# A hybrid decoder trunk: the weights' rings in a pool of their own, between the constants and the slots

## The chip, the core and the metric

The kernel runs on one core of a Trainium2 chip. The metric is the device time of one execution in microseconds (us), the median of several runs. All arithmetic is in float32 or in float32r, a form of float32 with fewer bits that most of its matmuls use.

## What is computed

Two layers over 512 tokens of width 1024. Each layer normalises x, projects it (indexer, attention, gated linear attention and pooling share one projection), mixes three branches, projects back, and runs a gated feed-forward block with a causal convolution of width 3. Cut to what matters here:

```python
def hybrid_layer(x, ...):
    h = rms_norm(x, norm1_g)
    proj = h @ w_in
    ...
    o_a = dsa_attention(qa, ka, va, qi, ki, wi)      # top 128 keys of an indexer, then softmax
    o_b = gla_chunked(qb, kb, vb, log_a)             # gated linear attention, norm, swish gate
    o_c = multiscale_pool(uc, w_pool, pool_scale)
    x = x + jnp.concatenate([o_a, o_b, o_c], axis=-1) @ w_out
    x = x + conv_glu_ffn(rms_norm(x, norm2_g), w_up, conv_w, conv_b, w_down)
    return x

def conv_glu_ffn(x, w_up, conv_w, conv_b, w_down):   # D_FF = 2816
    h = x @ w_up
    a, b = h[..., :D_FF], h[..., D_FF:]
    ...                                              # conv = causal convolution of a
    return (jax.nn.silu(conv) * b) @ w_down
```

By far the largest part of the arithmetic is the products with the weight matrices `w_in`, `w_out`, `w_up` and `w_down`, in two layers.

## The kernel before

Activations lie transposed: 128 partitions by 512 columns, one column per token, a tile (a "slot") for each 128 of the 1024 features. A product of full float32 precision is made of three float32r matmuls: weight and activation are each split into a high part and a remainder, and `mm3` issues high x high, high x remainder and remainder x high into the same PSUM bank. In the names of the profile the weights' parts are `hi` and `lo`; the activations' parts are `xh` and `xl`, or `h` and `l`. A row that says `mm<-xh,hi` is such a matmul. PSUM tiles `mm` take these products (four banks), tiles `aux` all smaller ones.

`Kern.weights` brings one weight block in: a DMA from the SP queue into `raw` (up to 1024 columns of 4 bytes in each partition), an ACT copy that rounds it to `hi`, and a DVE subtraction that makes `lo`. The three kinds of tile are rings: 3 buffers of `raw`, 5 of `hi`, 5 of `lo` (`NRAW`, `NW`). A block of 1024 columns is eight slices of 128 columns, so that a slice, 512 bytes in each partition, is what TensorE loads as its stationary operand:

```python
out.append((hi[:, kk, :].bitcast(F32R), lo[:, kk, :].bitcast(F32R)))
```

`Kern.chunk` then makes 128 output features of all 512 tokens: eight times `mm3`, with a weight slice stationary and a slot of 512 columns moving. `w_down` does the same inside `layer` and `finish`. In `Kern.tokens` (the value projection `w_v` and the 340 columns of `w_tok`) the roles are exchanged: a slice of the activations is stationary, and the weights move.

Only the first products of the first layer, `w_qi` and `w_gqk`, take their weights from another place: `run` loads them into ordinary slots, named `first` (raw), `fh` and `fl` (the parts), half as wide as the rings' tiles. Those slots have the same size as the slots of the activations.

The order of the work on each engine is made ahead by a planner in the kernel (`Plan.schedule`), from a cost for each operation, and written out. It knows tiles by name and by the number of buffers of their kind. It does not know addresses.

Where a tile lies in SBUF follows from the pools. A pool places its kinds of tile one after another, in the order of their first use, and the pools follow each other: `cst` (constants), then `sl` (everything else). The first constants start 128 bytes past a multiple of 512, and the pool's odd sizes end at 34,304 = 67 x 512. In `sl` come 50 slots of 2048 bytes, some small tiles, the four `tb` temporaries, two tiles `small` of 1344 bytes, and then the three rings, then the `ta` temporaries and the remaining small tiles. In bytes of a partition:

| tiles | start | past a multiple of 512 |
|---|---|---|
| slots (activations, `first`, `fh`, `fl`) | 34,304 | 0 |
| `raw` ring, 3 x 4096 | 152,960 | 384 |
| `hi` ring, 5 x 4096 | 165,248 | 384 |
| `lo` ring, 5 x 4096 | 185,728 | 384 |
| `ta` temporaries, 4 x 2048 | 206,208 | 384 |

So each weight slice of 512 bytes begins 384 bytes past a multiple of 512, and each slot at a multiple of 512.

Of the kernel before, what the change touches and what calls it, by code (L numbers as in the profile page):

```python
# [11 lines left out]
F32 = mybir.dt.float32  # L12
# [6 lines left out]
P = 128  # L19
# [75 lines left out]
NSLOT, NRAW, NW, NMM = 50, 3, 5, 4  # L95
# [21 lines left out]
class Op:  # L117
    __slots__ = ("eng", "cost", "calls", "preds", "succs", "tiles", "func", "tags", "port", "shapes")

    def __init__(self, eng):  # L120
        self.eng, self.cost, self.calls = eng, 0.0, []
        self.preds, self.succs, self.tiles, self.func, self.tags = {}, {}, set(), None, set()
        self.port, self.shapes = False, []
# [370 lines left out]
class Kern:  # L494
    def __init__(self, ctx, tc, a):
        self.tc, self.nc, self.a = tc, tc.nc, a
        e = ctx.enter_context
        self.pl = Plan(tc.nc)
        self.cst = e(tc.tile_pool(name="cst", bufs=1))
        self.sl = e(tc.tile_pool(name="sl", bufs=1))  # L500
        self.dr = e(tc.tile_pool(name="dr", bufs=1, space=bass.MemoryType.DRAM))
        self.ps = e(tc.tile_pool(name="ps", bufs=1, space=bass.MemoryType.PSUM))
        self.n = 0
# [29 lines left out]
    def weights(self, src, k, n, whole=False):  # L533
        nc = self.pl
        out = []
        step = k if whole else min((k + 1) // 2, 1104 // n)
        for k0 in range(0, k, step):
            kn = min(step, k - k0)
            raw = self.pl.tile(self.sl, NRAW, (P, kn * n), F32, "raw", self.nm("raw"))
            nc.sync.dma_start(out=raw, in_=src[:, k0 * n:(k0 + kn) * n])  # L540
            nc.in_turn("raw")
            hi = self.pl.tile(self.sl, NW, (P, kn, n), F32, "hi", self.nm("hi"))
            lo = self.pl.tile(self.sl, NW, (P, kn, n), F32, "lo", self.nm("lo"))
            hf = hi.rearrange("p k n -> p (k n)")
            lf = lo.rearrange("p k n -> p (k n)")
            nc.scalar.activation(out=hf.bitcast(F32R), in_=raw, func=AF.Copy)
            nc.in_turn("hi")
            nc.vector.tensor_tensor(out=lf.bitcast(F32R), in0=raw, in1=hf, op=OP.subtract)
            nc.in_turn("lo")
            for kk in range(kn):  # L550
                out.append((hi[:, kk, :].bitcast(F32R), lo[:, kk, :].bitcast(F32R)))
        return out
# [871 lines left out]
```

## Time and profile before

| | |
|---|---|
| median of 3 runs | 1260.47 us (1258.75 to 1262.89) |
| the profiled execution | 1258.48 us |
| its span, first to last instruction | 1256.7 us |
| mean granted TensorE clock | 0.997 of full |
| busy: TensorE matmul / VectorE / ScalarE / GpSimd | 99% / 55% / 40% / 26% |
| mean busy share of the DMA engines, hardware queue | 33.1% |

The span is the profiled execution without what lies before its first and after its last instruction, 1.8 us. A matmul's busy time in the profile overlaps that of the next one, and its end is modelled. What a stream of matmuls costs is therefore read from the distance between the starts of neighbours, called the pitch here, and not from the duration of one. All operations are recorded through one helper, so each has line 488, and rows are told apart by their tiles.

Roughly, the span goes: 0 to 31 us loading and the first products; 31 to 220 us attention, gated linear attention and pooling of layer 0, between them its projections; 220 to 640 us output projection and feed-forward block of layer 0; 640 to 840 us and 840 to 1220 us the same of layer 1; 1220 us to the end the last two feature blocks, the final norm and the output.

### The profile page before, as it was taken

How to read it: one execution, taken by the hardware profiler on the slowest of the kernel's cores; microseconds unless marked ns; L12 is line 12 of the kernel's file. 1: busy time of each engine (PE TensorE's matmuls, PEld its weight loads, DVE VectorE, ACT ScalarE, POOL GpSimd, SP SyncE). 2: the span in 40 equal slices, each digit the busy share in tenths (PEclk: the TensorE clock that was granted, in tenths of full speed). 3: DMA queues.
4: the chain of work that ended last, by engine and by line, in shares of the span. 5: the costliest groups of instructions: out<-in, count | busy, mean ns of one | idle time of the engine just before them, and what ended most of it. 6: DMA issues, size and time to landing. Idle time of an engine off the chain costs nothing.

```text
span 1256.7 us, 16776 instructions
## 1 busy us (share of the span) xinstructions
PE 1241.9 (99%) x6254; PEld 1004.3 (80%) x6254; DVE 695.5 (55%) x1256; ACT 508.6 (40%) x824; POOL 331.7 (26%) x281
## 2 busy tenths in 40 slices
PE   8999999999999999999999999999999999999997
PEld 7886678888888888888888777888888888888887
DVE  6569996355554245444357999644554524444333
ACT  6462278443332133333336324863433312333321
POOL 1363251222221022222108422512222200222211
PEclk9999999999999999999999999999999999999998
DMA  7322365122323323224343135432223223222322
GB/s 258 115 78 93 97 166 167 51 85 70 115 63 93 129 84 101 92 69 133 122 156 98 51 124 141 123 118 68 69 99 107 87 92 118 86 90 82 88 75 68
DMA packets 50561, 129.38 MB, mean 103 GB/s; under 512 B 7456, under 2 KB 10800, under 8 KB 50480
## 3 DMA queue, kind: packets, MB, share of 16 engines
q1 hardware_dynamic: 50368, 128.04, 33.1%
q8 instruction: 49, 0.80, 0.3%
q14 instruction: 32, 0.26, 0.1%
q0 software_dynamic: 112, 0.28, 0.1%
HBM read 109.22 MB, written 4.26 MB: 90 GB/s over the span
## 4 chain that ended last, share of the span: by engine, by line
PE 91%; DVE 5%; DMA 2%; issue 1%; ACT 1%; SPq 0%; POOL 0%; DVEq 0%
PE mm L488 81%; PE aux L488 10%; DVE score L488 1%; DVE lo L488 1%; DVE m L488 1%; DVE pl L488 1%; DMA raw<-in_w_tok 1%; DVE qt L488 1%; DMA x<-in_x 1%; SPq L488 0%; DMA raw<-in_w_rb 0%; DVE att L488 0%; DVE out L488 0%; ACT relu L488 0%; DVE u L488 0%
## 5 line engine op out<-in xcount | busy, mean ns | idle before, releaser
L488 PE MATMUL mm<-xh,hi 128*128 128x512 f32 x960 | 385.5, 402 | 0.3 <-DVE q L488 0.3
L488 PE MATMUL mm<-xh,lo 128*128 128x512 f32 x960 | 378.9, 395 | 0.0
L488 PE MATMUL mm<-xl,hi 128*128 128x512 f32 x960 | 378.6, 394 | 0.0
L488 DVE TENSOR_TENSOR lo<-raw,hi 128x1024 fp32r<-128x1024 f32 (+3 forms) x210 | 251.4, 1204 | 197.0 <-ACT hi L488 189.0
L488 ACT ACTIVATE hi<-raw 128x1024 fp32r<-128x1024 f32 (+3 forms) x210 | 203.2, 974 | 384.6 <-PE mm L488 333.4
L488 PEld LDWEIGHTS mm<-xh,hi 128*128 128x128 f32 x960 | 180.8, 188 | 47.6 <-issue 7.5
L488 PEld LDWEIGHTS mm<-xh,lo 128*128 128x128 f32 x960 | 180.7, 188 | 42.5
L488 PEld LDWEIGHTS mm<-xl,hi 128*128 128x128 f32 x960 | 180.9, 188 | 39.4 <-issue 0.2
L488 PE MATMUL mm<-h,hi 128*128 128x512 f32 (+2 forms) x492 | 187.8, 382 | 0.0
L488 PE MATMUL mm<-h,lo 128*128 128x512 f32 (+2 forms) x492 | 186.4, 379 | 0.0
L488 PE MATMUL mm<-l,hi 128*128 128x512 f32 (+2 forms) x492 | 186.3, 379 | 0.0
L488 POOL TENSOR_TENSOR cv<-cv,rstd 128x512 f32<-128x512 f32 x44 | 58.4, 1328 | 309.8 <-ACT cv L488 289.7
L488 POOL TENSOR_TENSOR l<-cv,h 128x512 fp32r<-128x512 f32 x44 | 70.4, 1600 | 157.0 <-ACT h L488 157.0
L488 PEld LDWEIGHTS mm<-h,lo 128*128 128x128 f32 x492 | 92.8, 189 | 18.8
L488 PEld LDWEIGHTS mm<-h,hi 128*128 128x128 f32 x492 | 92.8, 189 | 18.3 <-issue 0.3
L488 PEld LDWEIGHTS mm<-l,hi 128*128 128x128 f32 x492 | 92.9, 189 | 18.0
L488 DVE TENSOR_TENSOR x<-x,mm 128x512 f32<-128x512 f32 (+2 forms) x52 | 33.5, 646 | 103.0 <-PE mm L488 100.0
L488 DVE SCALAR_TENSOR_TENSOR cv<-a,vec,cv 128x511 f32<-128x511 f32 (+1 forms) x88 | 70.4, 806 | 33.5 <-ACT cv L488 32.2
L488 ACT ACTIVATE cv<-a,vec 128x512 f32<-128x512 f32 x44 | 35.6, 813 | 127.7 <-DVE a L488 127.7
L488 DVE TENSOR_TENSOR a<-mm,rstd 128x512 f32<-128x512 f32 x44 | 30.2, 691 | 96.6 <-PE mm L488 96.6
L488 POOL TENSOR_TENSOR sq<-sq,sq 128x512 f32<-128x512 f32 x23 | 34.6, 1506 | 151.2 <-ACT sq L488 151.1
L488 DVE TENSOR_TENSOR cv<-cv,mm 128x512 f32<-128x512 f32 x44 | 30.1, 685 | 41.1 <-PE mm L488 38.6
(199 smaller groups left out, 1393.5 us busy)
## 6 DMA issues: line engine op xcount, KB each, us to landing
raw<-in_w_up SPq DMA_DIRECT2D x88, 512.0 KB, 3.8
raw<-in_w_down SPq DMA_DIRECT2D x32, 384.0 KB, 3.1
raw<-in_w_down SPq DMA_DIRECT2D x32, 320.0 KB, 2.9
raw<-in_w_qk SPq DMA_DIRECT2D x16, 512.0 KB, 3.8
raw<-in_w_out SPq DMA_DIRECT2D x16, 512.0 KB, 4.0
x<-in_x SPq DMA_DIRECT2D x16, 256.0 KB, 6.0
raw<-in_w_v SPq DMA_DIRECT2D x8, 512.0 KB, 4.4
raw<-in_w_rb SPq DMA_DIRECT2D x4, 512.0 KB, 4.8
```

The lines of the kernel that those rows point to most:

```text
L488: self.issued(i, fn(*args, **kw))
```

## The change

The three rings are taken from a pool of their own, `wt`, which is opened between the constants' pool and the slots' pool. Nothing else is changed.

```diff
         self.cst = e(tc.tile_pool(name="cst", bufs=1))
+        self.wt = e(tc.tile_pool(name="wt", bufs=1))
         self.sl = e(tc.tile_pool(name="sl", bufs=1))
...
-            raw = self.pl.tile(self.sl, NRAW, (P, kn * n), F32, "raw", self.nm("raw"))
+            raw = self.pl.tile(self.wt, NRAW, (P, kn * n), F32, "raw", self.nm("raw"))
             nc.sync.dma_start(out=raw, in_=src[:, k0 * n:(k0 + kn) * n])
             nc.in_turn("raw")
-            hi = self.pl.tile(self.sl, NW, (P, kn, n), F32, "hi", self.nm("hi"))
-            lo = self.pl.tile(self.sl, NW, (P, kn, n), F32, "lo", self.nm("lo"))
+            hi = self.pl.tile(self.wt, NW, (P, kn, n), F32, "hi", self.nm("hi"))
+            lo = self.pl.tile(self.wt, NW, (P, kn, n), F32, "lo", self.nm("lo"))
```

The planner's input is the same, so the instructions of every engine stand in the same order as before, with the same waits. Only addresses change:

| tiles | start before | start after | past a multiple of 512, before and after |
|---|---|---|---|
| `raw` ring | 152,960 | 34,304 | 384, 0 |
| `hi` ring | 165,248 | 46,592 | 384, 0 |
| `lo` ring | 185,728 | 67,072 | 384, 0 |
| slots | 34,304 | 87,552 | 0, 0 |
| `tb` temporaries | 141,824 | 195,072 | 0, 0 |
| `ta` temporaries and the small tiles behind them | 206,208 | 206,208 | 384, 384 |

The rings take 53,248 bytes, which is 104 x 512 (and 26 x 2048), so what moves up behind them keeps its place within 512 bytes. The constants stay where they are. The `ta` temporaries stay 384 bytes past a multiple of 512. The slices of `w_tok` are 1360 bytes wide, so that of the three slices in a buffer only the first begins at a multiple of 512 after the change. The slices of all other weights do, whether they are 128, 256 or 512 columns wide.

## Rows read from the trace of the kernel before

**Rows 1.** The page's first part: busy time of each engine.

```profile
PE 1241.9 (99%) x6254; PEld 1004.3 (80%) x6254; DVE 695.5 (55%) x1256; ACT 508.6 (40%) x824; POOL 331.7 (26%) x281
```

**Rows 2.** The page's chain that ended last: shares by engine, then by line.

```profile
PE 91%; DVE 5%; DMA 2%; issue 1%; ACT 1%; SPq 0%; POOL 0%; DVEq 0%
PE mm L488 81%; PE aux L488 10%; DVE score L488 1%; DVE lo L488 1%; DVE m L488 1%; DVE pl L488 1%; DMA raw<-in_w_tok 1%; DVE qt L488 1%; DMA x<-in_x 1%; SPq L488 0%; DMA raw<-in_w_rb 0%; DVE att L488 0%; DVE out L488 0%; ACT relu L488 0%; DVE u L488 0%
```

**Rows 3.** The same chain in order of time: start us, us, what.

```profile
191.76 0.70 PE mm L488 x3
192.57 0.70 PE mm L488 x3
193.73 0.70 PE mm L488 x3
194.43 1.57 PE aux L488 x14
196.00 0.70 PE mm L488 x3
...
272.08 367.18 PE mm L488 x1590
```

**Rows 4.** Windows, mm tiles alone: stretch, length, busy (count touching it) by engine, clock, DMA.

```profile
13.00:21.60 8.60, 8.60 (x40) 7.12 (x39) 0.00 (x0) 0.00 (x0) 1.00 0.98 337
225.00:268.00 43.00, 43.00 (x186) 34.67 (x184) 5.48 (x8) 0.00 (x0) 1.00 0.19 62
273.00:633.00 360.00, 360.00 (x1551) 291.91 (x1550) 40.50 (x59) 0.00 (x0) 1.00 0.31 99
841.00:880.00 39.00, 39.00 (x169) 31.38 (x168) 5.38 (x8) 0.00 (x0) 1.00 0.26 81
884.00:1220.00 336.00, 335.42 (x1444) 271.98 (x1445) 37.75 (x55) 0.00 (x0) 1.00 0.29 91
31.00:220.00 189.00, 132.58 (x549) 96.80 (x549) 11.80 (x20) 4.59 (x8) 1.00 0.41 119
640.00:840.00 200.00, 142.20 (x579) 103.04 (x580) 11.67 (x20) 4.45 (x8) 1.00 0.38 110
```

**Rows 5.** Timeline of PE: start us, us, matmul; rows 1 to 3, 8, 9 and 43.

```profile
402.04 0.40 PE L488 MATMUL mm<-h,lo 128*128 128x512 f32 x1
402.28 0.40 PE L488 MATMUL mm<-h,hi 128*128 128x512 f32 x1
402.52 0.39 PE L488 MATMUL mm<-l,hi 128*128 128x512 f32 x1
...
403.67 0.40 PE L488 MATMUL mm<-h,hi 128*128 128x512 f32 x1
403.91 0.40 PE L488 MATMUL mm<-l,hi 128*128 128x512 f32 x1
...
411.80 0.40 PE L488 MATMUL mm<-h,lo 128*128 128x512 f32 x1
```

**Rows 6.** Timeline of PE, 849 to 854 us: the first and last of 18 rows.

```profile
849.75 0.40 PE L488 MATMUL mm<-xh,lo 128*128 128x512 f32 x1
...
853.72 0.39 PE L488 MATMUL mm<-l,hi 128*128 128x512 f32 x1
```

**Rows 7.** Timeline of PE, 13.3 to 21.5 us: the first and last of 37 rows.

```profile
13.30 0.39 PE L488 MATMUL mm<-xh,fl 128*128 128x512 f32 x1
...
21.46 0.39 PE L488 MATMUL mm<-xh,fl 128*128 128x512 f32 x1
```

**Rows 8.** Timeline of PE after a pause: four of 14 rows (the 1st, 2nd, 11th, 14th).

```profile
24.32 0.49 PE L488 MATMUL mm<-xh,fh 128*128 128x512 f32 x1
24.64 0.40 PE L488 MATMUL mm<-xl,fh 128*128 128x512 f32 x1
...
26.73 0.39 PE L488 MATMUL mm<-xl,fh 128*128 128x512 f32 x1
...
27.41 0.39 PE L488 MATMUL mm<-xl,fh 128*128 128x512 f32 x1
```

**Rows 9.** Groups by form on PE and ACT: xcount | busy us, mean ns | idle before.

```profile
L488 PE MATMUL mm<-xh,hi 128*128 128x512 f32 x960 | 385.5, 402 | 0.3 <-DVE q L488 0.3
L488 PE MATMUL mm<-h,hi 128*128 128x512 f32 x426 | 169.5, 398 | 0.0
L488 PE MATMUL mm<-hi,xh 128*128 128x512 f32 x64 | 26.0, 406 | 0.0
L488 ACT ACTIVATE hi<-raw 128x1024 fp32r<-128x1024 f32 x140 | 147.7, 1059 | 218.0 <-PE mm L488 185.1 <-issue 22.1 <-DMA raw<-in_w_rb 5.5
L488 ACT ACTIVATE hi<-raw 128x640 fp32r<-128x640 f32 x32 | 23.5, 735 | 90.3 <-PE mm L488 73.3 <-issue 16.9
```

**Rows 10.** Tile fh, the ACT copies: xcount: minimum/median/maximum ns.

```profile
L488 ACT ACTIVATE fh<-first x8: 615/617/632, 5.5 to 20.0; 128x512 fp32r<-128x512 f32 x8
```

**Rows 11.** Page, DVE's subtractions (all forms) and the commonest weight DMA.

```profile
L488 DVE TENSOR_TENSOR lo<-raw,hi 128x1024 fp32r<-128x1024 f32 (+3 forms) x210 | 251.4, 1204 | 197.0 <-ACT hi L488 189.0
raw<-in_w_up SPq DMA_DIRECT2D x88, 512.0 KB, 3.8
```

## The prediction

> **What bounds the kernel now.** First the busy times [rows 1]: TensorE is busy for 99% of the span, VectorE for 55%, ScalarE for 40%. A busy TensorE may still be waiting inside its pipeline, so the next view is the chain that ended last [rows 2]. It lies on TensorE for 91%, and 81% of it are the matmuls into the `mm` tiles, the products with the weights. In order of time [rows 3] one piece of that chain is 367.18 us long, 1590 matmuls with nothing between them. There the kernel takes as long as TensorE needs from one matmul to the next, and no other engine has a say. In the attention stretches the same rows show pieces of three matmuls, broken by small products.
>
> So the number to read is the pitch, start to start. The reader is to see three pitches for the same matmul, 128x512 in float32r:
>
> - In the feed-forward block [rows 5], 43 starts in a row span 402.04 to 411.80 us: 9.76 us by 42 is **232.4 ns**. The pitch is not even: 402.04 to 402.28 is 240, most others are 230, and 403.67 to 403.91 is 240 again. It returns every seventh matmul, while high and low parts change every third. Over the four long unbroken stretches [rows 4] it is the same: a count there holds about two matmuls that began before the stretch, so 360.00 us by 1549 is 232.4 and 43.00 by 185 is 232.4.
> - At 850 us [rows 6] the output projection of layer 1 runs at 3.97 us by 17, or 233.5 ns.
> - At the start, where the weights lie in ordinary slots as `fh` and `fl` [rows 7], 37 starts span 13.30 to 21.46 us: 8.16 us by 36 is **226.7 ns**, and that stretch is even.
>
> The rows rule out what would first come to mind. The granted clock is 1.00 in all of these stretches [rows 4], the 2.4 GHz level, so it is not the clock. In 13 to 21.6 us the DMA engines are 98% busy, in the others 19 to 32% [rows 4], so the faster stretch is the one with more traffic. What differs is the place: in the start stretch stationary and moving operand both begin at multiples of 512 bytes, and in the others the weights begin 384 bytes past one. A stream also has a warm-up [rows 8]: after a pause, nine pitches from 24.64 to 26.73 us average 232.2 ns, and then three to 27.41 us average 227. With both operands on the boundary a stream settles after some ten matmuls. With the weights off it, 1549 in a row do not settle.
>
> **The change part by part.** It removes, adds and reorders nothing on any engine or queue, SP's and GpSimd's included. It moves the rings from 384 past a multiple of 512 to 0, and the slots stay at 0. Four things touch the rings.
>
> *Matmuls in the long streams.* The weights' slices then lie as those of the start stretch do. I take its pitch. The four long stretches [rows 4] are 43 + 360 + 39 + 336 = 778 us at 232.4 ns (the third a little more). At 226.7 they would take 778 x 226.7 / 232.4 = 758.9, so 19.1 us less. All of it lies on the path, since the chain is TensorE there [rows 3]. The cover must hold: everything that feeds TensorE must come 2.5% sooner. VectorE has 45% of the span free and ScalarE 60% [rows 1], and a weight DMA lands in 3.8 us [rows 11], where the 48 matmuls of a block of `w_up` (two DMAs) take 48 x 226.7 ns = 10.9 us. Nothing is late next.
>
> The trace has no stream from the rings at a multiple of 512, so I bound this term. The least is 0 (the start stretch is faster for a reason that doesn't move with the rings), and the most is what all 128x512 matmuls of this kind could give. There are (960 + 426 + 64) x 3 = 4350 of them [rows 9], where each group stands for three; by 5.7 ns that is 24.8 us for this term and the next together. I take 19.1, the value of the stretch with the same layout.
>
> *Matmuls in the attention stretches.* There 132.58 + 142.20 = 274.8 us are `mm` work [rows 4]. At most 2.5% of it, 6.8 us, can go; at least 0. The streams there are short [rows 3], and a stream of fewer than ten is as slow with aligned operands [rows 8]. I take a quarter, 1.7 us.
>
> *ScalarE's and VectorE's work on the rings.* An ACT copy into `hi` takes 1059 ns for 1024 columns and 735 for 640 [rows 9], which by the slope of 0.84 ns a column is 627 for 512. The same copy between slots takes 617 [rows 10]. If those 10 ns go, 210 copies give 2 us of ScalarE, which is idle 60% of the time and hidden by TensorE. VectorE's 251.4 us of subtractions [rows 11] could move by as small a share either way, under the same cover. Zero for both. Without that cover, in the attention stretches, they'd be worth at most 2 us each.
>
> *DMAs into `raw`.* 3.8 us for 512 KB [rows 11]. DMA is 2% of the chain [rows 2], all at the start, so even 4% more or less of a transfer is below 1 us. Zero.
>
> Sum: 19.1 + 1.7 = 20.8 us. The profiled execution took 1258.48 us, so 1237.7. The median of the runs stands 2.0 us above that execution, so I forecast **1239.7 us**, 1.6% faster.
>
> **A rule that speaks against it.** The rows say that the pitch of one and the same instruction is 226.7 or 232.4 ns at one clock, and that the place of its operands is what I find different [rows 5, 7]. The Trainium skill, page "SBUF — State Buffer", section "Who interferes with whom", gives TensorE two independent SBUF read ports, one for the moving operand and one for weight loads, and says that PE and ACT never wait on anyone. By that no address could matter, the sum would be zero and the time 1260.5. The trace agrees so far that other engines' and DMA traffic makes no difference; two pitches at one clock are not explained by that rule.
>
> **The rivals.**
>
> *No change.* The start stretch is faster for another reason: it comes first, its weights sit close to the activations, or its tiles are half as wide. For it: there is only that one stretch, some 40 matmuls. Against it: inside 31 us the stream is broken and settles again [rows 8], and its slots are strewn among all the others. Time 1260.5. Chance 0.11. The rule of the Trainium skill above would give this time.
>
> *Half.* The 233.5 ns of [rows 6] show that a stream with the same alignment may settle into another pattern than [rows 5]. After the change a stream could settle at 226.7 in some blocks and stay at 232 in others after a pause. At half the gain, 1260.5 - 10.4 = 1250. Chance 0.08.
>
> *Slower.* Now the weight slices and the moving slots begin at the same place within 512 bytes, always. If the two reads of TensorE disturb each other when they run in step, every matmul takes the longer pitch that today comes once in seven, about 240 ns [rows 5]: 778 us x 240 / 232.4 is 25 us more, 1286. It decides as soon as the settled pitch is above 232.4. The start stretch speaks against it, since it has both operands in step and is the fastest [rows 7]. Chance 0.05.
>
> *The change does not do what it says.* The `ta` temporaries, `kt` and part of the constants stay off multiples of 512, so "all columns" is not true. But the long streams read only rings and slots. If `mm` streams were also slowed by others' temporaries, this is the half case.
>
> **How the numbers follow.** Forecast 0.76, half 0.08, no change 0.11, slower 0.05. The forecast's own range goes from 1235 (24.8 us less, 1235.7, and the scatter of the runs) to 1244 (the long streams alone, with a few microseconds lost after pauses). With the half case the range is 1235 to 1250, which leaves out 0.16. A measurement of this kernel can tell about 0.3%, or 3.8 us, from no change. Faster by more than that: 0.76 + 0.08 = 0.84, less 0.01 for halves that come to almost nothing, 0.83. Within: 0.11 + 0.01 = 0.12. Slower: 0.05.
>
> **What would show it.** In the changed kernel's timeline at 400 us, starts of neighbours should stand 226.7 ns apart, 42 pitches in 9.52 us, and evenly. The long piece of the chain, 1590 matmuls, should take about 358 us in place of 367. The stretch to 220 us should lose about 1 us. The ACT copies into `hi` should be some 10 ns shorter, if the address matters to them at all. The prediction is wrong if the pitch at 400 us is still 232, or uneven with another mean; then the start stretch had another reason. If the pitch falls but the time does not, something is late in the long streams, and the waits of TensorE would name it.

## The result, and the profile after

The changed kernel took **1241.48 us** (median of 4 runs, 1241.01 to 1242.22) beside 1260.72 us of the kernel before (4 runs): a ratio of 0.9848, 95% interval 0.983 to 0.9865. That is 1.5% or 19.2 us faster; the forecast was 1239.7 us. The profiled execution took 1241.71 us, with a span of 1240.0 us and a mean granted clock of 0.993. Of all executions in this document one, of the last kernel below, ran at a mean granted clock of 0.555, took 2034.37 us and is left out of its median.

**Where the time came from.** The first view to read is the timeline of TensorE at 400 us, the changed kernel, beside the uneven stream of [rows 5] (start us, us, matmul):

```profile
400.16 0.39 PE L488 MATMUL mm<-h,lo 128*128 128x512 f32 x1
400.38 0.39 PE L488 MATMUL mm<-h,hi 128*128 128x512 f32 x1
400.61 0.39 PE L488 MATMUL mm<-l,hi 128*128 128x512 f32 x1
400.84 0.39 PE L488 MATMUL mm<-h,lo 128*128 128x512 f32 x1
...
409.68 0.39 PE L488 MATMUL mm<-h,lo 128*128 128x512 f32 x1
```

From the first row to the last are 42 pitches in 9.52 us: 226.7 ns each, where [rows 5] gave 232.4. The starts are printed in steps of 10 ns, so 220 and 230 alternate; the 240 of before has gone. The windows, `mm` tiles alone, changed kernel, show the same over a long stretch and at an undisturbed clock. The columns, as in [rows 4], are stretch and length, then the busy time of TensorE's matmuls, its weight loads, VectorE and ScalarE, each with its count, then clock, DMA share and GB/s:

```profile
273.00:623.00 350.00, 350.00 (x1546) 289.75 (x1545) 40.44 (x59) 0.00 (x0) 1.00 0.32 101
```

With two matmuls taken off that began earlier, as in [rows 4], 350 us by 1544 is 226.7 ns; the kernel before would have 1506 in that time. The busy time of one row says little: in the groups by form the same matmul goes from 402 ns [rows 9] to

```profile
L488 PE MATMUL mm<-xh,hi 128*128 128x512 f32 x960 | 381.6, 397 | 0.5 <-DVE q L488 0.5
```

which is 5 ns less, of a time that overlaps the neighbour's. Starts are what count.

The chain in order of time gives each long stream as one piece. First the kernel before, with the pieces that [rows 3] does not show (start us, us, what):

```profile
224.08 44.13 PE mm L488 x189
...
835.26 45.68 PE mm L488 x195
884.82 342.77 PE mm L488 x1500
```

Then the changed kernel:

```profile
225.06 43.06 PE mm L488 x189
272.01 358.33 PE mm L488 x1590
827.97 44.43 PE mm L488 x195
876.28 334.58 PE mm L488 x1500
```

From these rows the whole difference of the two profiled executions can be laid out:

| stretch | how read | us |
|---|---|---|
| start and attention of layer 0 | first stream starts at 225.06, was 224.08 | +0.98 |
| first stream | 43.06 for 44.13 | -1.07 |
| second, layer 0's feed-forward block | 358.33 for 367.18 | -8.85 |
| attention of layer 1 | from the second stream's end to the third's start: 197.63 for 196.00 | +1.63 |
| third stream | 44.43 for 45.68 | -1.25 |
| fourth, layer 1's feed-forward block | 334.58 for 342.77 | -8.19 |
| the rest | | +0.05 |
| span | 1240.0 for 1256.7 | -16.7 |

The four streams give 19.4 us. The attention stretches, which should have given 1.7, took 2.6 more instead. The starts of the same matmuls, after against before, place this: 0.46 us is lost in the first 31 us, 1.04 at 141 to 150 us and 2.53 at 660 to 680 us, while the other parts gained about 1.4. What lies in the second and third place can be read. The windows of the two places, the kernel before (now all work; columns as in [rows 4], with GpSimd ahead of the clock):

```profile
136.00:150.00 14.00, 12.33 (x69) 7.73 (x68) 13.94 (x27) 3.97 (x6) 3.91 (x4) 1.00 0.29 85
660.00:690.00 30.00, 29.50 (x137) 24.14 (x136) 22.97 (x45) 19.67 (x29) 24.72 (x22) 1.00 0.35 102
```

And the changed kernel:

```profile
136.00:150.00 14.00, 12.32 (x64) 7.45 (x63) 13.43 (x26) 3.40 (x6) 3.26 (x3) 0.88 0.28 85
660.00:690.00 30.00, 28.44 (x128) 23.44 (x127) 19.08 (x50) 17.38 (x30) 20.41 (x20) 0.94 0.30 87
```

The granted clock is 0.88 and 0.94 in place of 1.00: in each place the records show one piece of 3.41 us at 0.5 (1.2 GHz), from 140.99 and from 670.05 us. A third such piece lies at 11.28 us; it put TensorE 1.4 us back, but this was made up by 31 us, where TensorE stands against the kernel before as it stood ahead of the piece, to within 0.2 us. The same holds in the two other traces with a piece there (the slots off, and everything on the boundary). The timeline of the changed kernel at the second place shows it, and a wait ahead of it (in brackets: the idle time, and what ended it):

```profile
667.90 0.35 PE L488 MATMUL aux<-l,sa 128*128 128x256 f32 x1 [0.84 <-POOL qb L488]
...
669.22 0.36 PE L488 MATMUL aux<-h,sa 128*128 128x256 f32 x1 [0.71 <-DMA sa<-sl]
...
671.21 0.63 PE L488 MATMUL mm<-lo,xh 128*128 128x512 f32 x1
671.63 0.63 PE L488 MATMUL mm<-hi,xl 128*128 128x512 f32 x1
672.06 0.63 PE L488 MATMUL mm<-hi,xh 128*128 128x512 f32 x1
```

TensorE idles 0.84 and 0.71 us, and a little later its matmuls start 0.43 us apart. At 141 us, too, it had idled just before, 1.68 us up to 140.69, and at 11 us 2.20 us up to 10.39. But idling alone does not settle it: the run at 256 bytes below idles 1.67 us at 140 us and the same 0.84 and 0.71 later, and its clock stays up. What it waits for at 667 us are the operands of layer 1's indexer scores: `sa`, the indexer's queries, and `l`, the remainder of its keys. (The first wait is put down to `qb`, but the DMA that copies `l`, issued at 665.61 us and with a median of 2.2 us to its landing, ends at about that time too.) They stand in the changed kernel's chain in order of time, behind `la`, `qb` and `qk` of the gated linear attention:

```profile
656.58 1.30 POOL la L488
657.87 0.93 POOL qb L488
...
659.82 0.97 POOL qk L488
...
661.07 1.04 POOL qb L488
662.11 1.25 POOL sl L488
663.37 2.22 POOL l L488
665.58 1.25 POOL sl L488
666.85 2.24 DMA sa<-sl
669.22 0.48 PE aux L488 x2
```

It is a series on GpSimd with a DMA at its end. TensorE did not overtake it: the series, too, began 8.85 us sooner than in the kernel before (`la` at 656.58 for 665.43 us). It is late because one instruction of it, the remainder `l` of the indexer's keys, took longer, while a subtraction of VectorE beside it took less time. The kernel before:

```profile
672.19 1.29 POOL L488 TENSOR_TENSOR l<-kg,h 64x512 fp32r<-64x512 f32 x1
672.21 4.59 DVE L488 TENSOR_TENSOR lo<-raw,hi 128x1024 fp32r<-128x1024 f32 x1 [4.39 <-ACT hi L488]
```

And the changed kernel:

```profile
663.07 1.37 DVE L488 TENSOR_TENSOR lo<-raw,hi 128x1024 fp32r<-128x1024 f32 x1 [4.12 <-ACT hi L488]
663.32 2.26 POOL L488 TENSOR_TENSOR l<-kg,h 64x512 fp32r<-64x512 f32 x1
```

From the start of `la` to the end of the last `sl` the series takes 10.24 us here and 9.29 there. So GpSimd is on the chain now, with 1% where [rows 2] have 0%; the changed kernel's page:

```profile
PE 89%; DVE 7%; DMA 1%; issue 1%; ACT 1%; POOL 1%; SPq 0%; DVEq 0%; POOLq 0%; ACTq 0%
```

The experiments show that the longer wait and the lower clock occur in kernels with the long pitch too, the lower clock less often.

### The profile page after: what moved, and what is told of

It reads as the page before. It is cut to its first block, busy times and chain, and to the rows that moved or that the text cites. A ratio compares the mean times of both kernels' runs of the same rounds, so it can differ in the third digit from the quotient of the medians.

```text
span 1240.0 us, 16776 instructions
## 1 busy us (share of the span) xinstructions
PE 1223.3 (99%) x6254; PEld 1003.7 (81%) x6254; DVE 692.6 (56%) x1256; ACT 508.2 (41%) x824; POOL 331.6 (27%) x281
## 4 chain that ended last, share of the span: by engine, by line
PE 89%; DVE 7%; DMA 1%; issue 1%; ACT 1%; POOL 1%; SPq 0%; DVEq 0%; POOLq 0%; ACTq 0%
PE mm L488 80%; PE aux L488 9%; DVE score L488 1%; DVE m L488 1%; DVE lo L488 1%; DVE qt L488 1%; DVE pl L488 1%; DMA x<-in_x 1%; DVE att L488 0%; DVE out L488 0%; SPq L488 0%; DMA s1l<-sl 0%; ACT L488 0%; POOL sl L488 0%; DVE st L488 0%
## 5 line engine op out<-in xcount | busy, mean ns | idle before, releaser
L488 PE MATMUL mm<-xh,hi 128*128 128x512 f32 x960 | 381.6, 397 | 0.5 <-DVE q L488 0.5
L488 PE MATMUL mm<-xl,hi 128*128 128x512 f32 x960 | 374.4, 390 | 0.0
L488 PE MATMUL mm<-xh,lo 128*128 128x512 f32 x960 | 374.3, 390 | 0.0
L488 DVE TENSOR_TENSOR lo<-raw,hi 128x1024 fp32r<-128x1024 f32 (+3 forms) x210 | 248.9, 1192 | 190.4 <-ACT hi L488 182.3
L488 PEld LDWEIGHTS mm<-h,lo 128*128 128x128 f32 x492 | 92.6, 188 | 16.7
L488 ACT ACTIVATE cv<-cv 128x512 f32<-128x512 f32 x44 | 27.6, 631 | 59.1 <-DVE cv L488 59.1
```

The source lines that it names most:

```text
L488: self.issued(i, fn(*args, **kw))
```

## The experiments

**The theory:** the pitch of back-to-back float32r matmuls depends on where the stationary and the moving operand begin in a partition. **The rivals:** the region of SBUF that the weights lie in, or their distance from the activations; the multiple of 512 as such; the copies and subtractions on the rings; and chance between executions. In all kernels the instructions, their order and their waits are those of the changed kernel, and nothing is left out. Only unused tiles shift addresses, by this helper:

```python
def pad(self, pool, size, tag):
    if tag not in self.pads:
        self.pads.add(tag)
        pool.tile([P, size // 4], F32, tag=tag, name=tag, bufs=1)
```

The **settled pitch** below is worked out from all starts: the mean pitch from the tenth matmul of an unbroken 128x512 stream on. It is 232.4 ns for the kernel before and 226.7 for the changed one. The row quoted for a kernel is always its window of 273 to 623 us, `mm` tiles alone; its first count, less two, is how many matmuls started in 350 us. (The busy time is below 350 where a break fell into the window, 349.35 for one of 0.65 us.)

### The kernel before, once more

No edit.

> The unchanged kernel, for a second trace of it. If its executions differ because a long stream settles into one pattern or another (232.4 ns a matmul in one trace, 233.5 at 850 us), this trace shows another share of the two patterns, and its time follows: each of the four long streams that runs at 233.3 in place of 232.4 adds 0.4% of its length, up to 3 us in all. If the scatter lies elsewhere, the pitches repeat the first trace stretch by stretch.

It took 1260.71 us, 2.2 more than the profiled execution of the kernel before, with the same settled pitch, 232.4 ns. Its span is 2.3 us longer, and the extra lies in two places. A clock of 0.5 for 3.41 us from 142.58 us costs 1.4 us, and the wait at the indexer scores, 1.52 us for 0.50 in the first trace, costs 1.0. In its timeline:

```profile
679.42 0.36 PE L488 MATMUL aux<-h,sa 128*128 128x256 f32 x1 [1.52 <-DMA sa<-sl]
```

So these two executions do not differ by the stream settling into another pattern, but by a wait and the clock. The first profiled execution of the kernel before had no such piece and the short wait, and stood 2.2 us under its median. The comparison of the two profiled executions (16.7 us) is therefore less than that of the medians (19.2 us).

### The rings where they were, on the boundary

The kernel before, with 128 bytes ahead of the rings and 384 behind them. The rings stay between slots and `ta`, at 153,088, 165,376 and 185,856, multiples of 512; `ta` stays at 384.

```diff
+            self.pad(self.sl, 128, "p_raw")
             raw = self.pl.tile(self.sl, NRAW, (P, kn * n), F32, "raw", self.nm("raw"))
...
             lo = self.pl.tile(self.sl, NW, (P, kn, n), F32, "lo", self.nm("lo"))
+            self.pad(self.sl, 384, "p_end")
```

> The rings stay where they were in the kernel before, behind the slots and the small tiles, moved up by 128 bytes alone, so that they begin at multiples of 512; 384 bytes behind them keep the ta temporaries 384 past a multiple of 512. Theory A (the place within 512 bytes decides): settled pitch 226.7 ns, time as after the change, 1241. Theory B (the low region, or nearness to the constants, decides): pitch 232.4, time 1260.

1242.47 us (4 runs, 1240.27 to 1243.26) beside 1259.3 us of before (13 runs): ratio 0.9859, 0.9843 to 0.9876. Settled pitch 226.7 ns.

```profile
273.00:623.00 350.00, 349.83 (x1543) 289.72 (x1544) 40.45 (x59) 0.00 (x0) 1.00 0.32 100
```

Two unused tiles do all that the new pool does. The region is not the cause.

### The rings in their new place, off the boundary

The changed kernel, with the rings 384 past a multiple of 512, as they were.

```diff
+            self.pad(self.wt, 384, "p_raw")
             raw = self.pl.tile(self.wt, NRAW, (P, kn * n), F32, "raw", self.nm("raw"))
...
             lo = self.pl.tile(self.wt, NW, (P, kn, n), F32, "lo", self.nm("lo"))
+            self.pad(self.wt, 128, "p_end")
```

> The changed kernel with 384 bytes ahead of the rings and 128 behind them: the rings lie in their new pool, low in SBUF, but begin 384 past a multiple of 512 as before. Theory A (the place within 512 bytes): pitch 232.4 ns, time 1260. Theory B (the region): 226.7, 1241.

1260.0 us (10 runs), ratio 0.9999, 0.999 to 1.0009: no difference from before. Settled pitch 232.4 ns.

```profile
273.00:623.00 350.00, 350.00 (x1508) 283.78 (x1507) 38.77 (x57) 0.00 (x0) 1.00 0.32 99
```

With the run above this closes it from both sides: the offset moves the time, the place does not.

### Only `raw` off

The changed kernel. `raw` begins 384 past a multiple of 512, `hi` and `lo` at one.

```diff
+            self.pad(self.wt, 384, "p_raw")
             raw = self.pl.tile(self.wt, NRAW, (P, kn * n), F32, "raw", self.nm("raw"))
...
+            self.pad(self.wt, 128, "p_hi")
             hi = self.pl.tile(self.wt, NW, (P, kn, n), F32, "hi", self.nm("hi"))
```

> The changed kernel with raw alone 384 past a multiple of 512, hi and lo at multiples. Raw is written by DMA and read by ScalarE and VectorE, never by TensorE. If the gain is TensorE's reading of its operands: pitch 226.7, time 1241 to 1242. If it came from the transfers or from the copies that read raw: the gain is lost, 1260; if in part, between.

1243.8 us in one execution, settled pitch 226.7 ns. The clock fell to 0.5 twice in this execution, for 6.83 us from 142.3 and for 3.41 us from 671.4, which is why it stands somewhat above the changed kernel's median. `raw`, which ScalarE, VectorE and the DMAs touch and TensorE doesn't, does not matter.

```profile
273.00:623.00 350.00, 349.35 (x1541) 289.13 (x1541) 40.45 (x59) 0.00 (x0) 1.00 0.32 100
```

### Only `lo` off

The changed kernel. `lo`, the stationary operand of every third matmul, begins 384 past.

```diff
+            self.pad(self.wt, 384, "p_lo")
             lo = self.pl.tile(self.wt, NW, (P, kn, n), F32, "lo", self.nm("lo"))
+            self.pad(self.wt, 128, "p_end")
```

> The changed kernel with the lo ring alone 384 past a multiple of 512; of the three matmuls of a product only the one with lo reads off the boundary. Theory A1 (each read off the boundary costs by itself): a third of the loss, settled pitch about 228.6 ns, time about 1248. Theory A2 (one late read upsets the stream, which then settles only if all reads are on the boundary): pitch 230 or more, uneven, 1252 to 1260. If lo does not matter: 226.7, 1241.

1258.78 us in one execution, settled pitch 231.1 ns: 4.4 of the 5.7 ns are lost where one matmul in three is off, not 1.9. The time says more than that, but part of it is the clock, which fell to 0.5 for 6.83 us from 142.1 and for 3.41 us from 678.0.

```profile
273.00:623.00 350.00, 349.35 (x1512) 285.75 (x1511) 39.11 (x57) 0.00 (x0) 1.00 0.31 98
```

Worked out from 866 starts between 400 and 600 us, the mean distance is 227 ns from a matmul `xh,hi` to the next, 233 from `xl,hi` to `xh,lo`, and 234 from `xh,lo` to the next `xh,hi`. The pairs in which both use `hi` keep the short pitch. Those into and out of `lo` do not, so an odd operand costs its neighbour too.

### Both operands off alike

The changed kernel. The rings and the slots all begin 384 past a multiple of 512 (`ta`, behind them, stays at 384).

```diff
+            self.pad(self.wt, 384, "p_raw")
             raw = self.pl.tile(self.wt, NRAW, (P, kn * n), F32, "raw", self.nm("raw"))
...
+        if tag == "ta":
+            self.pad(self.sl, 128, "p_ta")
```

> The changed kernel with rings and slots both moved by 384 bytes, so that stationary and moving operand both begin 384 past a multiple of 512 and lie alike; the ta temporaries stay as they were. Theory R (what counts is that the two operands lie alike): pitch 226.7, time 1241. Theory M (what counts is the multiple of 512 itself): pitch 232 or more, 1260 or more.

1244.5 us in one execution, settled pitch 226.7 ns (with clock drops at 142.7 and 671.8 us as in the run with `raw` off).

```profile
273.00:623.00 350.00, 349.35 (x1542) 289.20 (x1542) 40.42 (x59) 0.00 (x0) 1.00 0.32 100
```

This is the run that corrects the wording of the change: no operand of the long streams begins at a multiple of 512, and the gain is there. What counts is how the two lie relative to each other.

### Only the slots off

The changed kernel. The rings at multiples of 512, the slots 384 past.

```diff
+        self.pad(self.sl, 384, "p_sl")
         return self.pl.tile(self.sl, NSLOT
...
+        if tag == "ta":
+            self.pad(self.sl, 128, "p_ta")
```

> The changed kernel with the slots alone moved by 384 bytes: the weights' slices at multiples of 512, the activations 384 past one. In most matmuls the activations move, 2048 bytes each; in the value projection they are the stationary slices. Theory S (it is the 512-byte stationary slice that must not cross a multiple): long streams at 226.7, and only the value projection slower, time 1241 to 1243. Theory R (the operands must lie alike) and theory M for either operand: pitch 232, 1260.

1261.3 us in one execution, settled pitch 232.4 ns. It is the mirror of the kernel before, with the same loss.

```profile
273.00:623.00 350.00, 350.00 (x1507) 283.76 (x1507) 39.12 (x57) 0.00 (x0) 1.00 0.31 98
```

### Other distances: 256, 128, 64 and 32 bytes

The changed kernel with the slots at a multiple of 512 and the rings so many bytes past one. The edit for 256; the others have 128 and 384, 64 and 448, 32 and 480:

```diff
+            self.pad(self.wt, 256, "p_raw")
             raw = self.pl.tile(self.wt, NRAW, (P, kn * n), F32, "raw", self.nm("raw"))
...
             lo = self.pl.tile(self.wt, NW, (P, kn, n), F32, "lo", self.nm("lo"))
+            self.pad(self.wt, 256, "p_end")
```

> The changed kernel with the three rings 256 past a multiple of 512. If multiples of 256 are enough: pitch 226.7, 1241. If a slice must not cross a multiple of 512: about 232, 1260. If the loss grows with what is cut off at the boundary: between.

> The changed kernel with the three rings 128 past a multiple of 512, slots at multiples. By the runs so far two reads lie alike if their starts agree within 256 bytes (0 and 256 settle, 384 and 384 settle, 384 and 0 do not). Theory R256: 128 off is as bad as 384, pitch 232.4, time 1258 to 1261. If only the sign counts (the weights behind the slots, not ahead): 226.7 and 1238 to 1244.

> The changed kernel with the three rings 64 past a multiple of 512. Theory R256 in its strict form (any difference within 256 bytes upsets the stream): pitch about 232, 1258 to 1261. In its loose form (only a difference near half of 256 does): 226.7, 1238 to 1244. Between, if the loss grows with the difference: 229 to 230, about 1250.

> The changed kernel with the three rings 32 past a multiple of 512. Strict form of theory R256: about 232, 1258 to 1261. Loose form: 226.7, 1238 to 1244. If the loss grows with the difference: below that of 64, about 228, 1246.

256 bytes:

```profile
273.00:623.00 350.00, 350.00 (x1546) 289.80 (x1545) 39.14 (x57) 0.00 (x0) 1.00 0.32 102
```

128 bytes:

```profile
273.00:623.00 350.00, 349.56 (x1504) 283.46 (x1505) 39.12 (x57) 0.00 (x0) 1.00 0.31 98
```

64 bytes:

```profile
273.00:623.00 350.00, 350.00 (x1501) 282.01 (x1502) 39.12 (x57) 0.00 (x0) 1.00 0.31 97
```

32 bytes:

```profile
273.00:623.00 350.00, 350.00 (x1502) 282.01 (x1501) 39.07 (x57) 0.00 (x0) 1.00 0.31 98
```

| rings past the slots | settled pitch | time (one execution where no median is named) |
|---|---|---|
| 0 (the change) | 226.7 ns | 1241.48 us (median of 4) |
| 256 | 226.7 | 1238.19 |
| 384 (rings off) | 232.4 | 1260.0 (median of 10) |
| 128 | 232.4 | 1260.36 |
| 64 | 233.1 | 1263.41 |
| 32 | 233.3 | 1263.72 |

A distance of 256 is as good as none, and within 256 every distance that was tried costs 5.7 to 6.6 ns a matmul; the loss does not grow with the distance. (384 is 128 within 256. The 233.1 at 64 is a mean: the value projection, where the slots are stationary and the rings move, has 229, all others 233.3.)

The loss is one of matmuls with 512 columns. Worked out from the same starts and the operands' addresses, in unbroken streams of narrower float32r matmuls the pitch does not follow the distance: at 128 columns it is 111.2 ns for distances of 0, 32, 64 and 128 alike, at 256 columns 119.7 for 0 and 117.0 to 118.6 for the others, at 340 columns 154 to 160 without order.

The run at 256 is also the changed kernel without clock drops. The windows of 136 to 150 and 660 to 690 us, all work:

```profile
136.00:150.00 14.00, 12.08 (x68) 7.58 (x67) 13.96 (x28) 4.21 (x7) 3.62 (x3) 1.00 0.31 91
660.00:690.00 30.00, 28.44 (x136) 22.88 (x134) 23.09 (x58) 17.26 (x30) 19.19 (x20) 1.00 0.32 96
```

The wait at the indexer scores is there (0.84 and 0.71 us), the clock stays at 1.00, and the span is 1236.4 us, 3.6 under that of the changed kernel. Since drops come and go between executions, one execution is no evidence that 256 is better than 0.

### Everything of 512-byte columns on the boundary

The changed kernel, and the table of constants, `kt`, the rope tables, `ta` and the wide tiles behind it are brought to multiples of 512 too. It also gives one small tile two buffers for four, and allocates `mhalf` earlier.

```diff
+        self.pad(self.cst, 384, "p_cs")
         self.cs = self.const("consts", (P, _CONST.shape[1]))
...
         one = self.const("one", (P, 1))
+        self.mhalf = self.const("mhalf", (P, 8))
+        self.pad(self.cst, 128, "p_kt")
...
+        if tag == "ta":
+            self.pad(self.sl, 128, "p_ta")
...
-        self.rt = self.small(f"rt{n}", n)
+        self.rt = self.small(f"rt{n}", n, room=2 if n == 1 else 4)
```

> The changed kernel with the rest brought to multiples of 512 too: constants, kt, the rope tables, the wpl weights and the ta temporaries; mhalf is placed earlier and two small tiles have fewer buffers, the order of the work stays. If the small products of the attention part (10% of the chain before) also run faster on the boundary: each of the two attention stretches shorter by up to 1 us, time 1239 to 1240. If they are bound by something else: the same as the change, 1238 to 1243, with the same drops of the clock.

1239.40, 1239.85 and 1242.25 us. Ratio 0.9844, 0.9812 to 0.9876, and settled pitch 226.7 ns: not to be told from the change. The small products of the attention stretches don't give anything that can be measured, so no version was found that beats the change.

## Why the prediction was right

**The long streams: -19.1 us forecast, -19.4 measured** (1.07 + 8.85 + 1.25 + 8.19). The step that carried it was to look in the same trace for a stream of the same instruction with another layout [rows 7] and to take its pitch. Every settled stream of the changed kernel has that pitch, the output projection of layer 1 included, which stood at 233.5 [rows 6]. The long piece of the chain fell to 358.33 us, "about 358" in the forecast. One reading on the way was off: with two matmuls taken off, as for the other stretches, 43.00 us are 184 pitches and not 185, or 233.7 ns; by its starts that stream has 232.4, the value that was used.

**The attention stretches: -1.7 forecast, about -1.4 measured** in the parts without a drop of the clock or the wait. The quarter was a guess between 0 and 6.8, so that it came out this near is in part luck. With drops, wait and start the stretches took 2.6 us more in the profiled execution, and "the stretch to 220 us should lose about 1 us" did not show: it took 0.98 more, with 1.04 for the clock at 141 us and 0.46 for the start.

**ScalarE and VectorE: zero, right.** The guess beside it was wrong: ScalarE's copies are not 10 ns shorter. The groups by form of the changed kernel, beside 1059 and 735 ns in [rows 9]:

```profile
L488 ACT ACTIVATE hi<-raw 128x1024 fp32r<-128x1024 f32 x140 | 147.7, 1059 | 210.7 <-PE mm L488 175.6 <-issue 25.2 <-DMA raw<-in_w_rb 3.7
L488 ACT ACTIVATE hi<-raw 128x640 fp32r<-128x640 f32 x32 | 23.6, 736 | 87.3 <-PE mm L488 71.1 <-issue 16.1
```

So the 10 ns between the 627 drawn as a line through two widths and the 617 of [rows 10] are not the address. VectorE's subtraction took 1192 ns in the mean instead of 1204 [rows 11], and this is not the address either: the median of the 140 that are 1024 wide is 1225 ns in both traces, and the one subtraction shown above, 4.59 us and then 1.37, is worth 15 ns in a mean over 210. **DMAs: zero, right**; one into `raw` takes 3.9 us, was 3.8.

**"Nothing is late next" held where it was argued**, in the long streams. It was not asked of layer 1's attention stretch, and there the series on GpSimd and the DMA `sa<-sl` are late: all six traces with the short pitch have the waits of 0.84 to 0.88 and 0.70 to 0.72 us. But most with the long pitch wait there too, 1.46 to 1.52 us (the kernel before run again, the rings off in the new place, the slots off, 32 bytes) or in the two pieces (64 bytes, `lo` off). Only the first trace of the kernel before and that at 128 bytes have 0.50 us, for ScalarE. In these two the series takes 9.29 us, and VectorE's subtraction beside it 4.59; in the other twelve `l` or the `sl` behind it takes about 2.3 us in place of 1.3, the series 10.24 to 10.31, and the subtraction 1.2 to 2.4. That GpSimd and VectorE hold each other up there is what these rows suggest; no run tested it. So this wait, worth about 1.0 us, was there before in most executions and is not the work of the shorter pitch.

The clock was left out of the forecast, since [rows 4] show 1.00 throughout; one execution did not tell that it can fall in the attention stretches. It is lower after the change: the mean granted clock of the span averages 0.9961 over 21 executions of the kernel before and 0.9961 over the 10 with the rings off in the new place, but 0.9938 over the 4 of the changed kernel, 0.9940 over the 4 with the rings on the boundary in their old place and 0.9943 over 3 with everything on it. 0.0023 of 1240 us is 2.9 us of full clock. A drop of 3.41 us to 0.5 takes 1.7 us of it, and cost 1.04 us at 141 and about 1.5 at 670 us, so as an estimate 1.8 to 2.6 us went back that way, and less where the drop lies in the first 15 us, where it was made up. The forecast stood 1.8 us under the measured median, while the terms of its sum measured 20.8 us together, as forecast. That the clock is the whole of this rest is not shown: with the rings on the boundary in their old place the execution at 0.996 took 1240.27 us and the two at 0.993 took 1243.14 and 1243.26, but of the changed kernel the one at 0.996 took 1241.01 and the three at 0.993 1241.25 to 1242.22.

**The rivals.** *No change* supposed another reason for the fast start stretch: the two runs with the rings on the boundary in their old place and off it in the new one exclude the place, and the half-wide tiles are excluded by the rings' own streams at 226.7. The rule of the Trainium skill ("SBUF — State Buffer", "Who interferes with whom") that went with this rival holds here in one half: other traffic makes no difference (226.7 ns at a DMA share of 0.98 and of 0.32). Its two independent read ports do not fit these matmuls, since one and the same instruction has pitches of 226.7 and 232.4 to 233.3 ns by the addresses of its two operands. *Half* did not occur: every settled stream has the short pitch. *Slower* had it upside down: reads that lie alike are the good case. And the change is wider than its own reason: a multiple of 512 for "all columns" is enough but not needed.

**Shown:** the distance between the starts of stationary and moving operand within 256 bytes sets the pitch of these 128x512 matmuls, by the place of `hi`, `lo` and the slots, and not by that of `raw`. **Open:** what inside TensorE or SBUF makes a matmul wait, why the pitch takes the values 226.7, 232.4 and 233.1 to 233.3, why the clock falls, and more often with the short pitch, what lengthens `l` or `sl` on GpSimd, and which of the reads pays in the run with only `lo` off. Distances other than 0, 32, 64, 128, 256 and 384 were not tried for 512 columns, nor another type than float32r.

## What to carry to other kernels

Where float32r matmuls of 512 columns run back to back, let stationary and moving operand begin at the same place within 256 bytes, and look at the addresses after any pool with odd sizes: here two small unused tiles gave 1.4%. Read the pitch from start to start, not the busy time of one matmul, and look for a stream of the same instruction with another layout in the same trace before building anything. A few microseconds between two profiled executions may be a drop of the clock or a wait that comes and goes, so compare them stretch by stretch, and the mean granted clock over all executions, before explaining the sum.

## What was not expected of the hardware

- The loss is nearly all or nothing: operands 32 bytes apart cost 6.6 ns a matmul, 128 cost 5.7, 256 cost none. Matmuls of 128, 256 or 340 columns show no such loss.
- Both operands 384 bytes past a multiple of 512 are as good as both at one (226.7 ns each): no alignment as such is rewarded.
- One odd operand in three costs 4.4 of the 5.7 ns.
- TensorE's granted clock fell to 0.5 for 3.41 or 6.83 us at 11, at 141 to 143 or at 670 to 680 us in some executions and not in others. Counted in pieces of 3.41 us, the seven traces with the long pitch have 3, the six with the short one 14, and that with `lo` off 3; the short-pitch trace at 256 bytes has none. One piece in this kernel costs 1.0 to 1.5 us, and nothing that lasts at 11 us. (The last 6 to 9.5 us of every trace run at 0.5 too.)
- A GpSimd instruction of 1.3 us took 2.3 where a VectorE subtraction beside it took 1.2 to 2.4 (twelve traces), and kept to 1.3 where that took 4.59 (two).
